# Two hybrid attention layers on one core: input read in 2 KB rows and transposed raw, narrow first modulation blocks, low-rank inputs with features as rows

## The chip, the cores and the metric

The kernel runs on one core of a Trainium2 chip. The metric is device time in microseconds from the start to the end of one execution; less is better. The core has a matrix engine (TensorE, in the profile PE, with its weight loads as PEld), a vector engine (VectorE, DVE), a scalar engine (ScalarE, ACT), GpSimd (POOL), and SyncE (SP), whose queue issues nearly all DMA transfers here, strictly in order.

## What is computed

Two layers of a diffusion backbone over 512 latent tokens `x` and 256 context tokens `ctx`, 2048 features each. A layer modulates its normalised input, projects it once to all head groups and a gate, attends in three groups, and projects back. Cut to what matters:

```
shift, scale, gate = split(silu(c) @ w_ada[l] + b_ada[l], 3)        # also for c_ctx
h  = rms(x, norm_w[l]) * (1 + scale) + shift                          # 512 tokens
hc = rms(xc, norm_w[l]) * (1 + scale_c) + shift_c                     # 256 tokens
u  = h @ w_in[l]      # columns: qa ka va | qb kb vb | cq (768) ckv (512) kpe (64) | z (2048)
qc  = rms_heads(rms(cq, qa_norm) @ w_qb)
kvc = rms(ckv, kva_norm) @ w_kvb
o_a = neighbourhood attention, 8 heads x 64      (latent keys in a window + context keys)
o_b = sliding window, 12 query / 4 kv heads x 64 (sink logit, rotary)
o_c = latent attention, 6 heads, 128 + 64        (all keys)
x   = x + gate * ((concat(o_a, o_b, o_c) * silu(z)) @ w_out[l])
```

In layer 0 the context tokens go the same way, reading context keys alone; in layer 1 only the latent tokens are needed at the end, and so cq, the queries and the gate are computed for 512 tokens, keys and ckv for all 768. Everything is float32.

## The kernel before

**Arithmetic.** To reach float32 precision every matrix product is made of three matmuls of a reduced float type: each operand is split into a high part `hi` and a rest `lo`, and hi*hi, hi*lo, lo*hi are added in PSUM. ACT makes `hi` (a rounding copy), DVE makes `lo` (a subtraction). The helper `Kern.mm` (line 333) issues all of these matmuls, `Kern.tr` (336) all transposes by TensorE; the lines in the profile are those of such helpers (233 `act`, 239 `tt`, 254 and 256 `ts`, 261 `stt`, 266 `red`, 272 `ttr`, 277 `recip`, 282 `pmul`, 303 `start`, which issues a DMA on SP).

**The planner.** The program is written as many small strands (Python generators). A planner, `Weaver`, runs them in a virtual time `vt`, with estimated costs for every instruction, and the order in which it lets them issue is the order of the instructions on each engine and in SP's queue. Strands have priorities (0 goes first). Nothing of this runs on the chip; where an engine there is slower than planned, its instructions still come in the planned order, and a DMA whose buffer isn't free yet holds up all DMAs that stand behind it on SP.

**Memory.** A pool `s3` of 52 tiles (128 x 768) holds nearly all long-lived data: the residual `xk` (16 tiles, one per 128 features), the modulated input `hT` (hi and lo for each of the 16, so 32 tiles), queries, keys, values, staged parts of `w_ada`. `ws`/`wh`/`wl` (3, 3, 2 tiles of 128 x 512) hold weights as loaded, their hi part and their lo part; `tm` are temporaries; `g` are six PSUM banks and `S` two more for scores.

**Weights.** `Kern.loader` (priority 0) takes a free `ws` slot and issues the load of the next piece, `Kern.splitter` makes hi and lo, and a job takes them with `piece`. A `TJob` holds tokens as rows: for each k (128 input features) the stationary operand is a 128 x 128 block of h and 256 columns of weights move; a piece has two k. An `FJob` holds features as rows: a 128 x 128 block of weights is stationary and the tokens move, in two segments of 384 or one of 512; a piece has four k. Each waits, piece by piece, for the h it needs. A `Group` runs several jobs in turn, piece by piece.

**Start.** `load_x` and `load_xk` read x and ctx by feature blocks: for each k one DMA of 4 x 128 rows of 128 floats (512 bytes each) and one of 2 x 128 such rows. ACT squares the 768 columns, DVE sums them to `ssx`. When all 16 are there, `make_h` (once for the latent, once for the context tokens) computes 1/rms into `rx`, and `make_hk` multiplies each block by it (tokens are rows, so it is a scalar per row), transposes it, and, if the modulation for this k isn't known yet, copies it back to `xk`; when it is known, ACT computes hi, DVE or ACT the full value f = scale * x + shift, and DVE lo = f - hi.

The modulation needs `c @ w_ada` for shift and scale, 33.5 MB. `ada_blocks` loads it in DMAs of 256 KB for blocks of 256 columns (rows of 1 KB), shift and scale in turn, staged in up to 12 `s3` tiles; TensorE multiplies them (line 741) with the two columns c and c_ctx stationary, and `ada_finish` (758) transposes the result into place. The block for 256 columns gives two k. The weight loader starts when the first 8 of these loads have been issued. The gate's columns and all of layer 1's modulation follow later on DVE (`ada_vec`, lines 254 and 261, tile `ac`), spread over time.

**Projection.** Jobs for a layer are listed by hand at the end of `layer`. Layer 0 begins with the first half (k 0 to 7) of a key/value chunk and a query chunk of group A, then three gate jobs `zjob` for the heads of group C, then the second halves. A `kv_job` has two key heads and two value heads, a `q_job` up to four blocks of 64 columns: before, two query heads of A and two blocks of cq, or three query heads of B and one block of cq. Two more chunks hold ckv. After a chunk, `post_chunk` copies it from PSUM, squares and sums each 64-column block, applies the head norm (and the rotation for B) and transposes it. For the low-rank blocks ("c") it stores the sums in `ssc`, transposes the raw values and writes them to a DRAM scratch `cscr`.

**Low-rank stage.** `prep_C` reads `cscr` back, feature-major, and splits it with its gain into `cT` (hi, lo), three at a time, each when seven `s3` tiles are free; `prep_norm` computes the norms of cq and ckv from `ssc`. Then `w_qb` and `w_kvb` are applied (`post_qC`, `post_kvC`) and group C's attention runs, and then the output projection, whose `post_out` adds the residual, keeps `xk` for layer 1 and stores it to `xs1`. `free_h` gives back the 32 tiles of h after the last gate job. Attention units run in two worker strands beside the projections.

**Boundary of the layers.** `begin` starts `make_h` for layer 1 before the last output job (context tokens) of layer 0; the 1/rms needs the sums of all 16 blocks.

Of the kernel before, what the change touches and what calls it, by code (L numbers as in the profile page):

```python
# [139 lines left out]
class Kern:  # L140
# [96 lines left out]
    def tt(self, out, a, b, op):  # L237
        yield from self.gate("dve")
        self.nc.vector.tensor_tensor(out, a, b, op=op)  # L239
        self.w.bump("dve", 0.07 + 0.00104 * self.n(out))  # L240

# [133 lines left out]

    def loader(self, go):
# [52 lines left out]
class TJob:  # L429


    def __init__(self, K, W, runs, nk, tiles, lhs, evs, post, room=None, kpp=2, after=None, k0=0):
# [8 lines left out]
        self.inS = False  # L441
# [16 lines left out]
    def step(self, p):  # L458
# [9 lines left out]
        for b, ts in enumerate(self.banks):  # L468
# [8 lines left out]
            if self.evs is not None:  # L477
                yield from K.wait(*(e for x in self.evs[self.k0 + m * p:self.k0 + m * p + m] for e in pick(x, ts[0] < 4, ts[-1] >= 4)))
            yield from K.sync()
            ps = self.ps[b]  # L480
            for kk in range(m):
                k = m * p + kk
                for ti, t in enumerate(ts):
# [5 lines left out]
            K.w.pe(mmc(n) * 3 * m * len(ts))  # L489
# [34 lines left out]
class FJob:  # L524


    def __init__(self, K, W, c0, segs, rhs, evs, post, stack=False, room=None):
# [4 lines left out]
        self.inS = False  # L532
        self.done = [Event() for _ in segs]
# [12 lines left out]
    def step(self, p):  # L546
# [32 lines left out]
        K.drop(hi, lo)  # L579

# [34 lines left out]
def body(K):  # L615
# [8 lines left out]
    one = K.st([128, 1], name="one")  # L624
    nc.vector.memset(one, 1.0)
# [31 lines left out]
    ssc = K.st([128, 6, 20], name="ssc")  # L657
# [169 lines left out]
    def ada_scale(l, n, stag, ptag, depth, group):  # L827
        yield from ada_blocks(l, [(c + o, n) for c in range(0, D, n) for o in (0, D)], stag, ptag, depth, group)
# [20 lines left out]
    ev_x = [(Event(), Event()) for _ in range(KT)]  # L849
    hT = [[None] * KT, [None] * KT]  # L850

    def load_x():
        for k in range(KT):
            xk[k] = yield from K.get("s3")
            w.spawn(load_xk(k), 0)

    def load_xk(k):
        v = xk[k].rearrange("p (t f) -> p t f", f=128)
        yield from K.load(v[:, 0:4], t["x"][0, :, k * 128:(k + 1) * 128].rearrange("(t p) f -> p t f", p=128))
        yield from K.load(v[:, 4:6], t["ctx"][0, :, k * 128:(k + 1) * 128].rearrange("(t p) f -> p t f", p=128), 131072)  # L860
        sq = yield from K.get("s3")
        yield from K.act(sq, xk[k], AF.Square)
        yield from K.red(ssx[:, k, :], sq.rearrange("p (t f) -> p t f", f=128))
        K.put("s3", sq)
        K.set(ev_x[k][0])
        K.set(ev_x[k][1])

    def make_h(l, evs, ev_h, seg):

        a, b = ((0, 4), (4, 6))[seg]  # L870
        yield from K.wait(*(e[seg] for e in evs))
        tot = yield from sm()
        yield from K.red(tot[:, :b - a], ssx[:, :, a:b].rearrange("p k t -> p t k"))
        yield from K.rsqrt(rx[:, a:b], tot[:, :b - a], 1.0 / D)
        K.put("sm", tot)
        for k in range(KT):
            yield from K.token(("hl", "hc")[seg])
            w.spawn(make_hk(l, k, ev_h, seg, a, b), 2)
            yield None

    def make_hk(l, k, ev_h, seg, a, b):
        v = xk[k].rearrange("p (t f) -> p t f", f=128)
        c = slice(a * 128, b * 128)
        n = (b - a) * 128
        yield from K.mul(v[:, a:b], v[:, a:b], rx[:, a:b, None].to_broadcast([128, b - a, 128]))
# [5 lines left out]
        src = ps[:, :n]  # L891
        early = any(e.t is None for e in (ev_sh[l][k], ev_sc[l][k]))
        if early:
            yield from K.act(xk[k][:, c], src)
            src = xk[k][:, c]
            K.put("g", ps)
            K.put(("hl", "hc")[seg], 0)
        yield from K.wait(ev_sh[l][k], ev_sc[l][k])
# [8 lines left out]
        yield from K.act(hi, src, AF.Identity, scale=sc, bias=sh)  # L907
# [1239 lines left out]
```

## Time and profile before

| | |
|---|---|
| median of 3 runs | 2937.42 us (2935.22 to 2939.45) |
| the profiled execution | 2933.86 us, of which 2932.0 from the first to the last instruction (its span) |
| granted TensorE clock, mean | 0.989 |
| PE, PEld busy | 96%, 90% of the span |
| DVE, ACT, POOL busy | 69%, 42%, 5% |
| DMA | 350.09 MB, 119 GB/s over the span |
| costliest group | 7976 matmuls with `wh` moving, 1641.9 us busy (they overlap) |

Times of the views are in microseconds from the start of the span, unless marked ns. A busy matmul is a pipelined one: its duration is longer than the distance to the next, so rates are read from the distance between starts, or from stretches of the chain. PEld is the loading of the stationary operand. Where the profile names a tile, its number is left out: `g` is any of the six PSUM banks, `s` any tile of `s3`, and "L741 PE MATMUL g<-s,scT" is a modulation matmul. The chain is followed back from the last instruction: at each step to what released it.

### The profile page before, as it was taken

How to read it: one execution, taken by the hardware profiler on the slowest of the kernel's cores; microseconds unless marked ns; L12 is line 12 of the kernel's file. 1: busy time of each engine (PE TensorE's matmuls, PEld its weight loads, DVE VectorE, ACT ScalarE, POOL GpSimd, SP SyncE). 2: the span in 40 equal slices, each digit the busy share in tenths (PEclk: the TensorE clock that was granted, in tenths of full speed). 3: DMA queues.
4: the chain of work that ended last, by engine and by line, in shares of the span. 5: the costliest groups of instructions: out<-in, count | busy, mean ns of one | idle time of the engine just before them, and what ended most of it. 6: DMA issues, size and time to landing. Idle time of an engine off the chain costs nothing.

```text
span 2932.0 us, 54116 instructions
## 1 busy us (share of the span) xinstructions
PE 2808.8 (96%) x20218; PEld 2645.5 (90%) x20218; DVE 2013.5 (69%) x5277; ACT 1237.3 (42%) x2692; POOL 148.5 (5%) x221
## 2 busy tenths in 40 slices
PE   5999999999999999989999999999999999999998
PEld 3779999999999999979998789999998999889987
DVE  6247776676887878989964385666667686488643
ACT  5223443342543554546421263434444455356421
POOL 3000100000111001000000000000000000000000
PEclk9999999999999999999999999999999999999999
DMA  9764433433323234323443453444342423412253
GB/s 263 248 193 122 115 107 112 116 95 111 90 81 98 85 109 148 121 75 128 144 135 118 126 156 103 116 116 117 92 116 67 114 84 103 137 45 85 90 176 118
DMA packets 408119, 350.09 MB, mean 119 GB/s; under 512 B 66532, under 2 KB 336914, under 8 KB 407856
## 3 DMA queue, kind: packets, MB, share of 16 engines
q1 hardware_dynamic: 405984, 345.32, 39.6%
q8 instruction: 159, 2.61, 0.4%
q0 software_dynamic: 1872, 1.32, 0.4%
q14 instruction: 104, 0.85, 0.1%
HBM read 305.01 MB, written 32.07 MB: 115 GB/s over the span
## 4 chain that ended last, share of the span: by engine, by line
PE 79%; DVE 11%; DMA 5%; SPq 2%; issue 2%; ACT 2%; DVEq 0%; ACTq 0%
PE g L333 63%; PE S L333 9%; PE g L336 5%; DMA s<-w_ada 2%; SPq L303 2%; DVE s L239 2%; DVE wl L239 2%; DVE s L272 2%; DMA s<-scr 1%; ACT s L233 1%; DVE pt L239 1%; DVE ac L261 1%; DVE s L261 1%; DVE tm L239 1%; PE g L799 1%
## 5 line engine op out<-in xcount | busy, mean ns | idle before, releaser
L333 PE MATMUL g<-wh,s 128*128 128x256 f32 (+2 forms) x7976 | 1641.9, 295 | 15.7 <-DVE s L239 4.7
L333 PEld LDWEIGHTS g<-wh,s 128*128 128x128 f32 x7976 | 1303.6, 192 | 43.1 <-issue 10.0
L333 PE MATMUL g<-wl,s 128*128 128x256 f32 (+2 forms) x3988 | 1167.6, 293 | 5.3 <-DVE wl L239 5.2
L333 PEld LDWEIGHTS g<-wl,s 128*128 128x128 f32 x3988 | 767.0, 192 | 20.0 <-DVE wl L239 11.0
L239 DVE TENSOR_TENSOR wl<-ws,wh 128x512 fp32r<-128x512 f32 (+1 forms) x606 | 413.3, 683 | 490.2 <-PE g L333 292.8
L233 ACT ACTIVATE wh<-ws 128x512 fp32r<-128x512 f32 (+2 forms) x614 | 377.5, 616 | 450.5 <-PE g L333 393.8
L333 PE MATMUL g<-s,wh 128*128 128x384 f32 (+1 forms) x1600 | 451.2, 357 | 1.1 <-DVE s L239 0.6
L233 ACT ACTIVATE s<-s,sm 128x512 f32<-128x512 f32 (+3 forms) x260 | 192.5, 740 | 392.9 <-DVE sm L272 323.3
L261 DVE SCALAR_TENSOR_TENSOR ac<-wa,scT,ac 128x512 f32<-128x512 f32 x420 | 312.4, 761 | 6.8 <-DMA wa<-w_ada 6.2
L333 PEld LDWEIGHTS g<-s,wh 128*128 128x128 f32 x1600 | 293.3, 188 | 24.7 <-issue 2.1
L333 PE MATMUL g<-s,wl 128*128 128x384 f32 (+1 forms) x736 | 261.5, 355 | 0.1
L333 PE MATMUL S<-s,s 128*128 128x256 f32 (+3 forms) x1260 | 235.5, 316 | 13.7 <-DVE sm L272 11.0
L336 PE MATMUL g<-ident,s 128*128 128x128 f32 x1488 | 226.8, 279 | 16.7 <-DVE s L256 8.2
L233 ACT ACTIVATE tm<-g 128x512 f32<-128x512 f32 (+3 forms) x298 | 146.5, 513 | 211.6 <-PE g L333 127.9
L333 PE MATMUL g<-pt,s 128*128 128x256 f32 (+1 forms) x1348 | 217.4, 290 | 16.1 <-DVE pt L239 12.2
L239 DVE TENSOR_TENSOR pt<-g,pt 128x512 fp32r<-128x512 f32 (+1 forms) x306 | 187.6, 623 | 55.6 <-ACT pt L233 54.1
L233 ACT ACTIVATE pt<-g 128x512 fp32r<-128x512 f32 (+1 forms) x306 | 159.8, 543 | 128.4 <-PE g L336 122.9
L333 PEld LDWEIGHTS S<-s,s 128*128 128x128 f32 x1260 | 187.3, 192 | 29.6 <-DVE sm L272 17.5
L333 PEld LDWEIGHTS g<-pt,s 128*128 128x128 f32 x1348 | 186.4, 195 | 24.1 <-DVE pt L239 17.2
L336 PEld LDWEIGHTS g<-ident,s 128*128 128x128 f32 x1488 | 174.7, 143 | 31.9 <-DVE s L256 11.2
L282 POOL TENSOR_TENSOR s<-ot,s 64x256 f32<-64x256 f32 x100 | 87.2, 873 | 1471.9 <-DVE ot L239 1383.8
L333 PEld LDWEIGHTS g<-s,wl 128*128 128x128 f32 x736 | 138.9, 189 | 10.0 <-DVE wl L239 0.8
(156 smaller groups left out, 2483.7 us busy)
## 6 DMA issues: line engine op xcount, KB each, us to landing
wa<-w_ada SPq DMA_DIRECT2D x256, 256.0 KB
ws<-w_in SPq DMA_DIRECT2D x328, 128.0 KB
ws<-w_in SPq DMA_DIRECT2D x160, 256.0 KB
ws<-w_out SPq DMA_DIRECT2D x144, 256.0 KB
s<-w_ada SPq DMA_DIRECT2D x128, 256.0 KB
s<-scr SPq DMA_DIRECT2D x36, 384.0 KB
ws<-w_in SPq DMA_DIRECT2D x64, 192.0 KB
ws<-w_qb SPq DMA_DIRECT2D x54, 192.0 KB
```

The source lines that it names most:

```text
L233: self.nc.scalar.activation(out, in_, func, bias=bias, scale=scale, **kw)
L239: self.nc.vector.tensor_tensor(out, a, b, op=op)
L261: self.nc.vector.scalar_tensor_tensor(out, a, s, b, op0=op0, op1=op1)
L272: self.nc.vector.tensor_tensor_reduce(out, a, b, -1.0, init, OP.add, OP.min, acc)
L282: self.nc.gpsimd.tensor_tensor(out, a, b, op=OP.mult)
L303: self.nc.sync.dma_start(out, in_)
L333: self.nc.tensor.matmul(out, l, r, start=start, stop=stop, skip_group_check=True)
L336: self.nc.tensor.transpose(out, in_, self.ident)
L799: nc.tensor.matmul(pt[:, 2 * c + m:2 * c + m + 1], a[:, c * 128:(c + 1) * 128], one, start=c == 0 and m == sides[0], stop=c == n // 128 - ...
```

## The change

1. *Input.* `load_x` reads quarters of the features: for each quarter six DMAs of 128 tokens x 512 features (rows of 2 KB). ACT squares each with an accumulated sum into `ssx`; `turn_x` transposes the raw blocks and DVE copies them into `xk`, feature-major. `make_h` no longer multiplies before the transpose: it spreads 1/rms over all partitions (a diagonal matrix, multiplied by a matrix of ones on TensorE) into one `s3` tile R. `make_hk` is now f = x * scale * R (DVE), hi = f + shift (ACT), lo = f + shift - hi (DVE). In layer 1 `turn` transposes each block raw when its residual is there, before 1/rms is known.
2. *Modulation.* The first two blocks of 256 columns are cut in two blocks of 128 each (shift and scale), so k = 0 needs 8 loads, of 512-byte rows. The first two jobs of layer 0 wait for h one k at a time (`fine`).
3. *Loader.* While the first modulation runs, the planner places each weight load 2.5 us later (`margin`).
4. *Low-rank inputs.* cq and ckv leave the chunks. `cjob` projects 128 of their features with features as rows, like a gate job, and writes the result to `cscr` without a transpose. `prep_one` squares what it reads back, adds the squares over the feature blocks, and the new `prep_norm` sums them over partitions with one-column matmuls, for cq and ckv apart. Query chunks now hold four heads each (two jobs in A, three in B).
5. *Order.* The list of jobs is written out anew, with the ten `cjob`s between the chunks of groups A and B. `free_h` gives tiles back after each quarter of the last gate job. In `post_out` the store of the residual stands before the events that release the next layer.

```
-        yield from ada_blocks(l, [(c + o, n) for c in range(0, D, n) for o in (0, D)], stag, ptag, depth, group)
+        cols = [(0, 128), (128, 128)] + [(c, n) for c in range(n, D, n)]
+        yield from ada_blocks(l, [(c + o, n) for c, n in cols for o in (0, D)], stag, ptag, depth, group)
...
     def loader(self, go):
...
             s = yield from self.get("ws")
+            w.cur.ft += self.margin
             yield from sp["load"](s)
...
     def load_x():
+        for c in range(4):
+            st = []
+            for i in range(6):
+                x = yield from K.get("s3")
+                w.cur.ft = w.vt
+                src = t["x"][0, i * 128:(i + 1) * 128] if i < 4 else t["ctx"][0, i * 128 - 512:i * 128 - 384]
+                tx = yield from K.load_ahead(x[:, :512], src[:, c * 512:(c + 1) * 512])
+                st.append((x, tx))
+            w.spawn(use_x(c, st), 0)
...
     def make_hk(l, k, ev_h, seg, ev_t, tr):
...
-        yield from K.act(hi, src, AF.Identity, scale=sc, bias=sh)
...
-        yield from K.sub(lo, f[:, :n], r32(hi))
+        yield from K.stt(f[:, :n], xk[k][:, c], sc, bcast[l][1][:, c], OP.mult, OP.mult)
+        yield from K.act(hi, f[:, :n], AF.Identity, bias=sh)
+        yield from K.stt(lo, f[:, :n], sh, r32(hi), OP.add, OP.subtract)
...
-    def free_h():
-        for k in range(KT):
+    def free_h(p):
+
+        for k in range(4 * p, 4 * p + 4):
...
+        def cjob(f):
+
+            sg = segs if f < 6 or not last else [(0, 384), (384, 768)]
+
+            def post(ps, done):
+                for i, (a, b) in enumerate(sg):
+                    yield from K.wait(done[i])
+                    u = yield from K.get("tm")
+                    yield from K.act(u[:, :b - a], ps[i][:, :b - a])
+                    K.put("g", ps[i])
+                    yield from K.store(cscr[f * 128:(f + 1) * 128, a:b], u[:, :b - a], 512 * (b - a))
+                    K.put("tm", u)
+                K.set(ev_c[f])
+            return FJob(K, W, COL["cq"] + f * 128, sg, rhs_h, ev_h, post)
...
+        attA(0,1)
+        jobs.extend([zjob(1), kv_job(GA, "A", 2), cjob(6)])
+        attA(2,3)
+        jobs.extend([q_job(GA, "A", range(4, 8)), zjob(2), kv_job(GA, "A", 4)])
+        attA(4,5)
+        J(lambda: w.spawn(prep_B(), 1))
+        jobs.extend([cjob(7), kv_job(GA, "A", 6), zjob(3)])
+        attA(6,7)
+        jobs.extend([kv_job(GB, "B", 0), zjob(4), zjob(5), q_job(GB, "B", range(0, 4))])
+        attB(0,1,2,3)
+        jobs.extend([cjob(8), cjob(9), cjob(0), zjob(6), q_job(GB, "B", range(4, 8))])
+        attB(4,5)
+        jobs.extend([kv_job(GB, "B", 2), zjob(7)])
+        attB(6,7)
+        jobs.extend([cjob(1), zjob(8), cjob(2), q_job(GB, "B", range(8, 12)), zjob(9)])
+        attB(8,9,10,11)
+        jobs.extend([cjob(3), cjob(4), cjob(5)])
...
-        J(free_h)
+        jobs[-1].after = free_h
...
     def modulation():
         yield from ada_scale(0, 256, "s3", "g", 12, 4)
+        K.margin = 0.0
         w.spawn(ada_rest(), 5)
```

More of the change, by code (lines that the diff above doesn't have):

```diff
@@ L579, in step @@
         K.drop(hi, lo)
+        if self.after is not None:
+            self.after(p)
     def run(self):
@@ L864, in load_xk @@
         K.put("s3", sq)
[L865 to L879, printed above, removed]
@@ L881, in make_hk, with turn_x @@
-    def make_hk(l, k, ev_h, seg, a, b):
+        for e in ev_x[c]:
+            K.set(e)
+    def turn_x(k, seg, st, left):
+        a, b = SEG[seg]
+        w.cur.ft = max(tx for _, tx in st[a:b])
+        yield from K.token(("hl", "hc")[seg])
+        ps = yield from K.get("g")
+        yield from K.sync()
+        o = k % 4 * 128
+        for i in range(a, b):
+            K.tr(ps[:, (i - a) * 128:(i - a + 1) * 128], st[i][0][:, o:o + 128])
+        w.pe(0.109 * (b - a))
+        left[seg] -= 1
+        if left[seg] == 0:
+            K.put("s3", *(x for x, _ in st[a:b]))
+        yield from K.copy(xk[k][:, a * 128:b * 128], ps[:, :(b - a) * 128])
+        K.put("g", ps)
+        K.put(("hl", "hc")[seg], 0)
+        K.set(ev_t0[k][seg])
@@ L882, in make_hk, with turn @@
+    SEG = ((0, 4), (4, 6))
+    bcast = {}
+    def turn(l, k, seg, ev, ev_t):
+        a, b = SEG[seg]
+        yield from K.wait(ev)
+        yield from K.token(("hl", "hc")[seg])
         v = xk[k].rearrange("p (t f) -> p t f", f=128)
         c = slice(a * 128, b * 128)
[L884 to L885 removed]
         ps = yield from K.get("g")
@@ L1615, in prep_one, with prep_norm @@
             K.put("ck", 0)
+            yield from K.act(raw[:, :n], raw[:, :n], AF.Square)
+            if f == 0:
+                squares[key] = raw
+            else:
+                yield from K.wait(ev_sq[key, f - 1])
+                yield from K.add(squares[key][:, :n], squares[key][:, :n], raw[:, :n])
+                K.put("s3", raw)
+            K.set(ev_sq[key, f])
+            if f == nf - 1:
+                w.spawn(prep_norm(key, n // 128), 2, w.cur.ft)
+        def prep_norm(key, nt):
+            q = squares[key]
+            ps = yield from K.get("g")
+            yield from K.sync()
+            for ti in range(nt):
+                nc.tensor.matmul(ps[:, ti:ti + 1], q[:, ti * 128:(ti + 1) * 128], one, start=ti == 0, stop=ti == nt - 1,
+                                 skip_group_check=True)
+            w.pe(0.22 * nt)
+            K.put("s3", q)
+            if key == "q":
+                yield from K.ts(rq_eps[:, 0:nt], ps[:, 0:nt], 1.0 / 768, OP.mult, EPS, OP.add)
+                yield from K.ts(rq_eps[:, 0:nt], rq_eps[:, 0:nt], EPS, OP.mult)
+                K.set(ev_rq)
+            else:
+                yield from K.rsqrt(rkv, ps[:, 0:6], 1.0 / 512)
+                K.set(ev_rkv)
+            K.put("g", ps)
         def room_qC(p):
```

226 lines of the change are left out of this document (114 added, 112 removed).

## The prediction

> **What bounds the kernel now.** I read the page first: the engine totals and the chain that ended last.
>
> ```profile
> PE 2808.8 (96%) x20218; PEld 2645.5 (90%) x20218; DVE 2013.5 (69%) x5277; ACT 1237.3 (42%) x2692; POOL 148.5 (5%) x221
> PE 79%; DVE 11%; DMA 5%; SPq 2%; issue 2%; ACT 2%; DVEq 0%; ACTq 0%
> ```
>
> TensorE carries 79% of the chain. So a saving is either matmul time taken off TensorE, or a stretch in which TensorE stood waiting. The second kind is found by stage (columns: stretch, its length, then PE, PEld, DVE, ACT, POOL busy, granted clock, DMA share, GB/s).
>
> ```profile
> 0.00:50.00 50.00, 17.07 (x135) 11.29 (x135) 33.13 (x75) 26.16 (x48) 21.68 (x43) 1.00 1.01 274
> 100.00:150.00 50.00, 47.37 (x368) 37.57 (x367) 15.93 (x36) 16.59 (x30) 0.00 (x0) 1.00 0.74 230
> 150.00:200.00 50.00, 44.17 (x306) 33.30 (x305) 20.16 (x44) 12.85 (x25) 0.30 (x2) 0.97 0.70 220
> 200.00:250.00 50.00, 50.00 (x380) 49.97 (x379) 27.98 (x58) 10.47 (x22) 0.00 (x0) 1.00 0.42 122
> 800.00:850.00 50.00, 43.93 (x260) 40.80 (x261) 42.56 (x138) 25.51 (x72) 6.68 (x7) 0.86 0.21 61
> 1150.00:1200.00 50.00, 45.11 (x265) 42.93 (x264) 37.80 (x89) 24.04 (x49) 8.12 (x15) 0.93 0.63 193
> 2200.00:2250.00 50.00, 46.29 (x348) 44.45 (x348) 37.65 (x109) 24.83 (x65) 2.92 (x4) 0.93 0.23 67
> ```
>
> From 200 us on TensorE is full, and it loses a few microseconds only at stage changes (800, 1150, 2200). The first 200 us are different: weight loads (PEld) fill 34 to 38 of 50 us there, against 50 afterwards. Since TensorE is full behind this stretch, a microsecond won in it should stay won.
>
> **1. The low-rank inputs (cjob).** The 1280 columns of cq and ckv are now computed in token-major chunks (256 columns moving, 16 x 3 matmuls for each 128 tokens). Layer 0 has 5 such chunks' worth, 5 x 16 x 3 x 6 = 1440 matmuls; layer 1 has 3 for four token tiles and 2 for six, 1152. These 2592 go. In their place stand feature-major jobs: 10 in layer 0 and 4 in layer 1 with two pieces of 384 tokens, 14 x 96 = 1344 matmuls, and 6 in layer 1 with 512 tokens, 288. Prices from stretches of the chain in which TensorE ran one shape after another (start, length, what):
>
> ```profile
> 270.58 2.88 PE g L333 x24
> 311.69 4.17 PE g L333 x24
> 2486.39 54.60 PE g L333 x238
> 825.29 0.87 PE g L336 x8
> ```
>
> 24 matmuls of 256 columns in 2.88 us are 0.120 each, 384 columns 4.17/24 = 0.174, 512 columns 54.60/238 = 0.229, a transpose 0.87/8 = 0.109. So 2592 x 0.120 = 311.0 becomes 1344 x 0.174 + 288 x 0.229 = 299.8: 11.2 us less. The Trainium skill's "TensorE: Matmul & The Clock Gate", section "Wait — 56ns, not 53.3ns?", has a fixed cost of only about 2.5 ns per warm matmul. By its figures the same exchange would be worth an estimated 2.5 us; the three rows here show about 13 ns above 2.4 columns per ns, so the measurement decides.
>
> The transposes of the raw chunk go as well: 10 column blocks x 6 tiles in layer 0, 6 x 4 + 4 x 6 in layer 1, 108 x 0.109 = 11.8 us. The norms return as one-column matmuls (6 + 6 + 6 + 4 = 22), priced by the first row below; the 12 matmuls that spread 1/rms over the partitions have no like, so they lie between the first row (0.116) and the second (9.9/32 = 0.31).
>
> ```profile
> L799 PE MATMUL g<-one,ac 128*128 128x1 f32 x224 | 26.0, 244 | 0.0
> L1394 PE MATMUL g<-tm,flip 128*128 128x256 f32 x32 | 9.9, 389 | 2.3 <-DMA tm<-scr 1.2 <-DMA ws<-w_in 1.0
> ```
>
> 22 x 0.116 = 2.6, and I take the dearer end for the six of layer 1, 1.9; layer 0's six fall where TensorE is idle. TensorE's work falls by 11.2 + 11.8 - 4.5 = **18.5 us**. It counts in full where TensorE is the bound, which the row from 200 us shows; where DVE is the limit (the 800 row) it could be worth half, so 10 to 19.
>
> **2. The start.** The rows that mark it, from the timeline of TensorE (start, length, what, idle before):
>
> ```profile
> 31.89 3.14 PE L741 MATMUL g<-s,scT 128*32 128x256 f32 x16 [22.20 <-DMA s<-w_ada]
> 56.05 0.39 PE L333 MATMUL g<-wh,s 128*128 128x256 f32 x1
> 183.57 0.61 PE L758 MATMUL g<-sel,tm 128*128 128x2 f32 x4 [0.48 <-ACT tm L233]
> ```
>
> Modulation starts at 31.9 us, the first projection at 56.1, and the last modulation block ends at 183.6. What TensorE did between 56 and 184 us, by shape (first and last group of each; 256 columns: 4 groups, 288 matmuls; 384 columns: 4 groups, 216):
>
> ```profile
> L741 PE MATMUL g<-s,scT 128*32 128x256 f32 x418 | 36.5, 394 | 4.5 <-DMA s<-w_ada 3.7
> L333 PE MATMUL g<-s,wh 128*128 128x384 f32 x96 | 27.0, 345 | 0.0
> L333 PE MATMUL g<-wh,s 128*128 128x256 f32 x128 | 26.8, 295 | 2.2 <-DVE s L239 1.2 <-ACT s L233 1.0
> L333 PE MATMUL S<-wl,s 128*128 128x256 f32 x32 | 9.0, 282 | 0.0
> L333 PE MATMUL S<-s,wl 128*128 128x384 f32 x24 | 8.0, 334 | 0.0
> ```
>
> and one group of modulation from the chain of waits:
>
> ```profile
> 120.84 1.00 PE g L741 x16
> ```
>
> With 1.00/16 = 0.0625 for a modulation matmul the work is 288 x 0.120 + 216 x 0.174 + 418 x 0.0625 = 98.3 us of 128: about 30 us of gaps. The projections of the last four k can't run before the last block, so the end of modulation is what moves everything later. It is set by the loads (the stages; the waits of SP's queue up to 200 us: total, times, longest; the DMA issues):
>
> ```profile
> 4.00:26.00 22.00, 1.27 (x5) 0.88 (x5) 10.79 (x13) 11.99 (x19) 13.93 (x27) 1.00 1.05 248
> 30.00:60.00 30.00, 25.67 (x228) 17.32 (x229) 26.30 (x79) 19.09 (x42) 4.57 (x8) 1.00 1.08 337
> 60.00:180.00 120.00, 111.97 (x935) 86.80 (x933) 36.41 (x83) 32.58 (x60) 0.00 (x0) 0.99 0.79 245
> ```
>
> ```profile
> SPq L303 <- DVE wl L239: 45.4, 15, 6.2
> ```
>
> ```profile
> s<-x SPq DMA_DIRECT2D x16, 256.0 KB
> s<-ctx SPq DMA_DIRECT2D x16, 128.0 KB
> ```
>
> The input in 512-byte rows came at 248 GB/s, w_ada mostly in 1 KB rows at 337. The input is 16 x 384 KB = 6.29 MB: 25.4 us at the one rate, 18.7 at the other, so 2 KB rows give about 6.7 (nothing to 8 if they are no faster, or faster still). The narrow first blocks turn 4.2 MB of w_ada into 512-byte rows: 16.9 instead of 12.4 us, 4.5 back. Net 2.2. The Trainium skill's "DMA: Bandwidth & Descriptors", section "Specifications", calls 512 B enough for line rate; by it both terms are nil and the sum is 2.2 us poorer. The rows disagree.
>
> From 60 to 180 us the engines were 79% busy at 245 GB/s. At 337 the same bytes take 87 us: 33 us are lost. The named cause is in the SP row: 15 waits before 200 us, 45.4 us in all, 3.0 each, where a weight load stood at the head of SP's queue for a slot that DVE had not yet split, with w_ada loads behind it. The margin places each weight load 2.5 us later in the plan, so w_ada loads go ahead of it. That can take away at most 15 x 2.5 = 37 us of waits. I take half of the 33, since the 12 staging slots are emptied by TensorE, which is itself at 98 of 128 us: 16.3. **The start: 2.2 + 16.3 = 18.5 us**, between 0 (the waits remain) and 33. Narrow blocks and single-k steps let the first projection begin near 38 us instead of 56: 18.7 for the input, 8 loads of 2.1 MB at 248 GB/s, some 10 for start and the chain of small operations. That fills TensorE earlier, but counts only if the end of modulation comes forward too.
>
> The margin also delays the weights, and TensorE waits for them. Its cover: a piece feeds 4.2 us of matmuls (24 at 0.174, or 36 at 0.120), three slots 12.5 us, of which the margin takes 2.5 and leaves 10 for load and split. Without that cover each of the 28 pieces of this stage could cost 2.5. The single-k step adds a wait on TensorE for every k; behind it in the queue stand the next modulation matmuls, which the pair of k would have held up longer: 0.
>
> **3. Freeing h in quarters.** At the low-rank stage the chain holds
>
> ```profile
> 1159.27 7.45 DMA s<-scr
> ```
>
> a read back of cq that could be issued only when the last gate job gave its 32 tiles up at once. Freed by quarters over a job of about 16 us, three more reads start earlier: **7.5 us**, layer 0 only (0 to 8). The squares moved here (10 of 768 columns per layer on ACT, 9 adds on DVE) lie beside the next round's matmuls; the 1150 row has DVE busy 38 of 50 us. The evictions of the first query round now wait for the query inputs' own norm, after the sixth square; behind them TensorE waits only for the accumulators of a third round, and has 54 matmuls (9.4 us) of the second to do first. Without that cover the last square, add and small matmuls cost 3.
>
> **4. The layer boundary.** There DVE is full and makes h:
>
> ```profile
> 1720.00:1730.00 10.00, 9.16 (x68) 8.44 (x67) 10.00 (x27) 7.23 (x14) 0.00 (x0) 1.00 0.40 111
> L239 DVE TENSOR_TENSOR s<-s,s 128x512 fp32r<-128x512 f32 x16 | 11.0, 687 | 0.9 <-ACT s L233 0.9
> L261 DVE SCALAR_TENSOR_TENSOR ac<-wa,scT,ac 128x512 f32<-128x512 f32 x420 | 312.4, 761 | 6.8 <-DMA wa<-w_ada 6.2
> ```
>
> Two plain 512-column operations per k (0.69 each) become two with a scalar (0.76): 16 x 0.15 = 2.4 us, and 1/rms must first be spread. Against this, transposes run raw before the norm is known, while TensorE waits for the last output chunks. I put it at 0, from -5 to +5. The residual stores move ahead of the event, not ahead of other loads of the same post: 0.
>
> **Sum:** 18.5 + 18.5 + 7.5 = 44.5 us. The profiled execution took 2933.86 (span 2932.0 plus 1.9), so 2889.4; the median of the runs shown is 3.6 higher, hence **2893**.
>
> **The rivals.**
> A. *The start does not get shorter.* SP waits follow how far the chip lags behind the plan; if TensorE and the staging slots set the pace, 2.5 us only moves the waits. For it: waits of up to 6.2 us. Then 2937.4 - 18.5 - 7.5 = 2911. Chance 0.17.
> B. *The start reaches its limit*, loads at 337 GB/s throughout (33 + 2.2), and the stalls at 800 and 2200 us go as group B gets more projection work beside it: about 5 each by the PE column. 2937.4 - 18.5 - 35 - 7.5 - 10 = 2866. Chance 0.13.
> C. *Slower: hand-offs in group B.* Four query heads now come from one job, so four heads' attention is released at once, on DVE. At 800 us one such hand-off cost 6 us of TensorE and a clock of 0.86 over 50 us (7 more): 13. With four hand-offs in each layer so hit, 8 x 13 less the two there now is +78, and the result 2937.4 - 44.5 + 78 = 2971. It decides from four extra stalls. Against it: the new order puts four feature-major jobs, some 67 us, behind the first of them. Chance 0.10.
> D. *The low-rank change is no saving*, the matmuls removed having been beside DVE work anyway, and half the start: 2937.4 - 9 = 2928. Chance 0.05.
>
> **How the numbers follow.** Forecast 0.55, its own range 2878 to 2908. The range for 8 in 10 takes in A and most of the way to B: 2868 to 2922. A measurement here tells 0.2% (6 us) from no change. Faster: forecast, A, B and most of D, 0.87; same 0.04; slower 0.09.
>
> **What would show it.** Right: the first projection near 38 us and the last modulation block at 160 to 170; SP waits for the split well under 45 us before 200; no 256-column chunk of cq; the 7.45 us read gone from the chain near 1100; projections running at 0.174 for the new jobs. Wrong: DMA still near 245 GB/s after 60 us (A), or a PE column below 45 at several places of group B (C).

## The result, and the profile after

The changed kernel takes 2905.89 us (median of four runs, 2902.42 to 2908.11), the kernel before 2936.53 beside it (four runs, 2935.22 to 2939.45). The ratio is 0.9893, 95% interval 0.9876 to 0.991. The profiled execution took 2902.42 us, its span 2900.6. The forecast was 2893 and, for the span, 44.5 us less than before; the span is 31.4 us shorter.

The page after, engine totals and chain shares:

```profile
PE 2794.6 (96%) x19282; PEld 2625.2 (91%) x19282; DVE 1996.1 (69%) x5106; ACT 1199.7 (41%) x2642; POOL 145.8 (5%) x217
PE 78%; DVE 11%; DMA 6%; issue 2%; ACT 2%; SPq 1%; DVEq 0%; ACTq 0%
```

TensorE issues 936 instructions less, and its share of the span is what it was. The stretches that were shown of before, in the same columns:

```profile
100.00:150.00 50.00, 48.48 (x389) 41.51 (x390) 18.36 (x38) 16.84 (x32) 0.00 (x0) 1.00 0.80 247
150.00:200.00 50.00, 45.98 (x321) 38.21 (x320) 23.81 (x45) 12.65 (x25) 0.30 (x2) 0.93 0.57 179
800.00:850.00 50.00, 46.64 (x344) 45.47 (x343) 46.69 (x135) 24.38 (x64) 5.22 (x7) 1.00 0.28 82
1150.00:1200.00 50.00, 47.04 (x315) 44.27 (x314) 48.39 (x152) 29.69 (x76) 0.00 (x0) 1.00 0.41 123
2200.00:2250.00 50.00, 50.00 (x422) 50.00 (x421) 37.33 (x99) 20.51 (x49) 6.30 (x6) 1.00 0.32 91
4.00:26.00 22.00, 14.12 (x76) 11.10 (x77) 11.51 (x24) 14.35 (x45) 12.55 (x24) 0.90 0.96 268
60.00:180.00 120.00, 110.70 (x937) 88.10 (x937) 45.03 (x94) 32.91 (x63) 0.00 (x0) 0.97 0.82 256
```

At 2200 us the loss is gone (PE 46.3 to 50.0); at 800 us 3.4 us of 6.1 are left (PE 43.9 to 46.6), with the clock at 1.00 instead of 0.86. The start's rates have hardly moved: 256 GB/s from 60 to 180 us where there were 245, and the input in 2 KB rows comes at 268 GB/s where there were 248. (e1 and e11 below read the input as before, at 219 and 220 GB/s in the same stretch, so the gain there is 8 to 22%.) TensorE's timeline, and the waits of SP up to 200 us:

```profile
35.85 2.90 PE L958 MATMUL g<-tm,ones 128*128 128x128 f32 x12 [1.19 <-DVE tm L239]
44.52 0.58 PE L338 MATMUL g<-wh,s 128*128 128x256 f32 x1
171.40 1.74 PE L758 MATMUL g<-s,scT 128*32 128x256 f32 x8 [1.50 <-DMA s<-w_ada]
```

```profile
SPq L308 <- DVE wl L239: 38.6, 13, 7.1
```

The first projection begins at 44.5 us (56.1 before), the last modulation matmul starts at 172.5 (182.7). Thirteen waits of SP for a split weight are left, 38.6 us, where there were 15 and 45.4. That fall is no finding: e5 to e9 and e12 run the same instructions up to here and have 39.2 to 45.9 us in 12 or 13 waits. The chain says what the last load of the modulation stood behind:

```profile
162.07 2.19 DVE s L266 x4
164.70 0.62 ACT wh L233
165.35 0.70 DVE wl L239
166.07 0.37 SPq L308
166.49 4.87 DMA s<-w_ada
171.40 1.77 PE g L758 x8
```

VectorE works on h (four operations), then ACT makes the high part of a weight and VectorE its rest, and only then does SP come past the weight load to the `w_ada` load behind it. The wait that the margin was to take away is still the last one.

For the rest the span is cut at four events of SP's and TensorE's timelines: the start of the last modulation matmul of layer 0, the issue of the last load of `w_in`, of `w_kvb` and of `w_out` of layer 0, and of the last load of `w_in` of layer 1. The columns are the lengths between them (us, one profiled execution each).

| kernel | start | projections 0 | low-rank 0 | output 0 | projections 1 | rest | span |
|---|---|---|---|---|---|---|---|
| before | 182.7 | 954.4 | 209.7 | 361.1 | 823.0 | 401.1 | 2932.0 |
| after | 172.5 | 934.0 | 205.9 | 376.2 | 811.6 | 400.4 | 2900.6 |
| e1, low-rank alone | 183.0 | 933.9 | 206.6 | 365.8 | 812.7 | 398.3 | 2900.3 |
| e2, start alone | 174.1 | 956.3 | 212.1 | 368.5 | 814.9 | 401.5 | 2927.3 |
| e3, no margin | 182.7 | 936.9 | 203.8 | 375.6 | 811.3 | 399.1 | 2909.5 |
| e5, old h in layer 1 | 175.6 | 936.9 | 205.5 | 365.8 | 810.5 | 398.1 | 2892.3 |
| e7, h freed at the end | 175.8 | 932.3 | 206.7 | 366.2 | 810.5 | 400.0 | 2891.6 |
| e8, `cjob`s last | 172.9 | 971.1 | 199.6 | 369.4 | 838.1 | 407.6 | 2958.7 |
| e9, e5 and e7 | 177.7 | 937.4 | 200.9 | 357.2 | 809.9 | 397.4 | 2880.6 |
| e11, e1, h freed at the end | 183.7 | 934.7 | 204.8 | 356.8 | 813.8 | 398.2 | 2892.0 |
| e12, e7, late transposes | 176.2 | 936.1 | 204.4 | 358.3 | 815.0 | 399.7 | 2889.7 |

After against before: 10.2 won in the start, 20.4 and 11.4 in the projections, 3.8 in the low-rank stage, 0.7 in the rest, and **15.1 lost in the output stage of layer 0**, on which the prediction had put nothing: 31.4. The start column scatters: after, e5, e7, e8, e9 and e12 are alike up to there and lie from 172.5 to 177.7. So do the others: e7, e9 and e12 hold the same instructions into the output stage, and have 932.3 to 937.4 us in projections 0 and 200.9 to 206.7 in the low-rank stage. A difference of some 5 us in one cell shows nothing by itself.

### The profile page after: what moved, and what is told of

Same layout as the page of the kernel before. It is cut to its first block, busy times and chain, and to the rows that moved or that the text cites. A ratio compares the mean times of both kernels' runs of the same rounds, so it can differ in the third digit from the quotient of the medians.

```text
span 2900.6 us, 51642 instructions
## 1 busy us (share of the span) xinstructions
PE 2794.6 (96%) x19282; PEld 2625.2 (91%) x19282; DVE 1996.1 (69%) x5106; ACT 1199.7 (41%) x2642; POOL 145.8 (5%) x217
## 4 chain that ended last, share of the span: by engine, by line
PE 78%; DVE 11%; DMA 6%; issue 2%; ACT 2%; SPq 1%; DVEq 0%; ACTq 0%
PE g L338 62%; PE S L338 9%; PE g L341 5%; DVE s L266 2%; DVE wl L239 2%; DVE s L239 2%; DVE s L277 1%; DMA s<-scr 1%; ACT s L233 1%; DMA tm<-scr 1%; DVE ac L266 1%; DVE tm L239 1%; SPq L308 1%; PE g L758 1%; PE g L816 1%
## 5 line engine op out<-in xcount | busy, mean ns | idle before, releaser
L338 PE MATMUL g<-wh,s 128*128 128x256 f32 (+2 forms) x6248 | 1312.9, 299 | 17.0 <-DVE s L266 4.7
L338 PEld LDWEIGHTS g<-wh,s 128*128 128x128 f32 x6248 | 1029.1, 193 | 46.1 <-ACT s L233 8.5
L338 PE MATMUL g<-wl,s 128*128 128x256 f32 (+2 forms) x3124 | 924.5, 296 | 5.4 <-DVE wl L239 5.4
L338 PE MATMUL g<-s,wh 128*128 128x384 f32 (+1 forms) x2688 | 763.2, 355 | 0.6 <-ACT wh L233 0.5
L338 PEld LDWEIGHTS g<-wl,s 128*128 128x128 f32 x3124 | 603.3, 193 | 18.1 <-DVE wl L239 9.1
L338 PEld LDWEIGHTS g<-s,wh 128*128 128x128 f32 x2688 | 493.0, 188 | 31.2 <-issue 2.1
L338 PE MATMUL g<-s,wl 128*128 128x384 f32 (+1 forms) x1280 | 449.1, 351 | 0.3 <-DVE wl L239 0.3
L338 PEld LDWEIGHTS g<-s,wl 128*128 128x128 f32 x1280 | 241.4, 189 | 12.7 <-DVE wl L239 0.9
L338 PE MATMUL g<-pt,s 128*128 128x256 f32 (+1 forms) x1348 | 210.4, 286 | 9.5 <-DVE pt L239 5.5
L239 DVE TENSOR_TENSOR pt<-g,pt 128x512 fp32r<-128x512 f32 (+1 forms) x306 | 187.5, 623 | 45.4 <-ACT pt L233 43.5
L341 PEld LDWEIGHTS g<-ident,s 128*128 128x128 f32 x1488 | 176.5, 143 | 37.1 <-DVE s L261 6.3
L233 ACT ACTIVATE tm<-g 128x384 f32<-128x384 f32 (+4 forms) x240 | 113.4, 491 | 206.6 <-PE g L338 129.6
```

Source lines behind the costliest of these rows:

```text
L233: self.nc.scalar.activation(out, in_, func, bias=bias, scale=scale, **kw)
L338: self.nc.tensor.matmul(out, l, r, start=start, stop=stop, skip_group_check=True)
L341: self.nc.tensor.transpose(out, in_, self.ident)
```

## The experiments

The theory after the result: the low-rank part does what it was meant to do and more; the start gives less than forecast; and the output stage loses time to the boundary between the layers, where the raw transposes stand and VectorE has more to do. The rivals: the loss is the new order of the jobs, or the freeing by quarters, or the start's lead is swallowed by some later wait in any case. Kernels that didn't run side by side are compared by their ratios to the kernel before, taken on the same chip.

**e1, the low-rank part alone, and e2, all the rest.** e1 keeps parts 4 and 5 of the change (new jobs and order, quarters) and has input, modulation, margin, h and the residual's store as before; e2 is the complement. Lines of e1 against the whole change:

```
-        self.margin = 2.5
-        cols = [(0, 128), (128, 128)] + [(c, n) for c in range(n, D, n)]
-        yield from K.stt(f[:, :n], xk[k][:, c], sc, bcast[l][1][:, c], OP.mult, OP.mult)
+        yield from K.mul(v[:, a:b], v[:, a:b], rx[:, a:b, None].to_broadcast([128, b - a, 128]))
```

> Only the low-rank jobs, the new order and the freeing by quarters; input, modulation, loader and the making of h as before. By stages of the two profiles the projections of layer 0, the low-rank stage and layer 1 without its boundary gained about 35 us, the start 10, and output projection with boundary lost 14. If these parts add up, this kernel takes 2936.5 - 35 = about 2901, no slower than the whole change. The rival, that the low-rank part gave only the 18.5 + 7.5 of the prediction and the start the rest, expects 2910.

> The complement: new input, narrow blocks, single-k waits, margin, h made with a spread 1/rms in both layers, residual store earlier; low-rank blocks and order as before. If the start's 10 us are given back at the boundary, within 5 us of the kernel before (2932 to 2942). If the start pays by itself as predicted (18.5, boundary 0), 2918. The last modulation block should end near 172 us either way.

e1: 2903.74 us, ratio 0.9904 (0.9882 to 0.9926). e2: 2929.81, ratio 0.9987 (0.9978 to 0.9996). So the low-rank part alone is as fast as the whole change, as far as these intervals tell, and the rest alone is worth about 0.1%. By the table e2 has won 8.6 us when the modulation ends, and loses 7.4 in the output stage of layer 0; the whole change stands 11.1 ahead of e1 at the last load of `w_kvb` (172.5 + 934.0 + 205.9 = 1312.4 against 1323.5) and 0.6 ahead at the last load of `w_out`. The lead is lost inside one stage.

**e3, the margin, and e4, the narrow blocks.**

```
-        self.margin = 2.5
+        self.margin = 0.0
```

```
-        cols = [(0, 128), (128, 128)] + [(c, n) for c in range(n, D, n)]
+        cols = [(c, n) for c in range(0, D, n)]
```

> The whole change with margin 0. If the margin takes SP's waits away, as predicted, the last modulation block ends about 10 us later than the 172 us of the whole change, and the time is 2914 to 2918. If it only moves the waits (they fell from 45.4 to 38.6 us before 200 us), the time stays within 4 us of 2906.

> The whole change with first modulation blocks 256 columns wide. If 512-byte rows of w_ada cost what the prediction took (4.5 us on the end of modulation), this kernel is 2 to 5 us faster, 2901 to 2904. If the early first projection (44.5 us instead of 56.1) is what the start gained, it is 5 to 8 slower, 2911 to 2914.

e3: 2908.74 us, ratio 0.9916 (0.9898 to 0.9934). The last modulation matmul starts at 182.7 again, as before the change and as was expected if the margin works; the time is not the 2914 to 2918 that went with it, and its interval overlaps that of the whole change. SP's waits:

```profile
SPq L308 <- DVE wl L239: 46.4, 15, 7.1
```

So in the profile all that the start won is the margin's; 2 KB rows and narrow blocks alone bring the first projection to 44.1 us and the end of the modulation nowhere. But the margin doesn't win by taking these waits away: 46.4 us here is within 1 us of the 45.9 that e9 has with the margin, and e9's modulation still ends 5 us earlier. What the later weight loads change instead was not traced. e4: 2905.45, ratio 0.9907 (0.9891 to 0.9923), the first projection at 47.8 us and the modulation's end at 174.4, inside the scatter: the narrow blocks can't be told from nothing.

**e5, layer 1's h as before.** Layer 1 multiplies by 1/rms before the transposes again, after the last output chunk of its tokens; ACT makes hi and f from PSUM.

```
-                w.spawn(make_h(l, ev_in[l], ev_h, seg), 2)
+                w.spawn((make_h1 if l else make_h)(l, ev_in[l], ev_h, seg), 2)
```

> The whole change, but layer 1 makes h as before (multiplied, then transposed, f on ACT). In the whole change DVE is full for 40 us at the boundary (10.00 of 10) and TensorE drops to 5.94 of 10 with a clock of 0.84. If this is what took the start's gain back, the stall goes and the kernel is 8 to 11 us faster than 2905.9, 2895 to 2898. If the boundary costs nothing, as the prediction had it, it stays within 4 us.

2888.81 us, ratio 0.9846 (0.983 to 0.9861), against 0.9893 (0.9876 to 0.991) of the whole change: the boundary cost the difference of the ratios, 0.0047 or 13.8 us (by the two intervals, give or take 7). The output stage is down from 376.2 to 365.8.

**e6, the copies of the context's transposes on ACT** instead of VectorE.

```
-        if seg == 0:
-            yield from K.act(xk[k][:, c], ps)
-        else:
-            yield from K.copy(xk[k][:, c], ps[:, :256])
+        yield from K.act(xk[k][:, c], ps[:, :(b - a) * 128])
```

> The whole change; in layer 1 the 16 copies of the context blocks (0.42 us each on DVE) are made by ACT, which is half idle there. If DVE's time alone sets the boundary, 16 x 0.42 = 6.7 us less DVE work, of which the part that falls into the full 40 us (8 of 16 copies, 3.3 us) is won: 2902 to 2904. If the order of DVE's work or the wait for the norm sets it: 2906.

2899.39 us, ratio 0.9885 (0.9869 to 0.9902). That interval overlaps the whole change's in nearly all its width; the run decides nothing.

**e7, h's tiles given back after the last gate job,** as before.

```
-        jobs[-1].after = free_h
+        J(lambda: [free_h(p) for p in range(4)] and None)
```

> The whole change with h's 32 tiles given back after the last gate job, as before. The prediction took 7.5 us for freeing by quarters, so 2913. By the stages of the two profiles the low-rank stage of layer 0 was 3.9 us shorter: 2910. If the read back was hidden by other work in any case: 2906.

2893.29 us, ratio 0.986 (0.9846 to 0.9875): giving the tiles back *later* is faster, by 0.0033 or 9.7 us (give or take 7). In the low-rank stage the chain of e7 holds reads of the scratch again,

```profile
1129.93 5.26 DMA s<-scr
1138.60 10.69 DMA s<-scr
```

which the chain of the changed kernel has not in that stage. So the freeing does take the read away, and the stage is no shorter for it: 205.9 and 205.5 us with quarters (after, e5), 206.7, 200.9 and 204.4 without (e7, e9, e12). The price stands in the next stage, 376.2 us against 366.2, in two places. The changed kernel, in the columns of the stretches, 0 to 30 and 180 to 210 us after the stage's begin:

```profile
1312.40:1342.40 30.00, 27.55 (x197) 26.09 (x196) 27.79 (x81) 18.89 (x42) 1.07 (x2) 0.94 0.37 116
1492.40:1522.40 30.00, 24.50 (x155) 23.32 (x155) 20.66 (x39) 5.46 (x8) 0.00 (x0) 0.77 0.47 136
```

and e7:

```profile
1314.80:1344.80 30.00, 30.00 (x233) 28.95 (x232) 29.55 (x90) 20.59 (x52) 1.06 (x2) 1.00 0.42 125
1494.80:1524.80 30.00, 26.45 (x205) 25.66 (x204) 25.83 (x48) 8.09 (x12) 0.00 (x0) 0.94 0.53 161
```

36 matmuls less in the first 30 us, 50 less in the second. Nothing of what runs there was edited; the freed tiles let the planner start other strands earlier, and from the low-rank stage on the same instructions stand in another order. The changed kernel's second place, in its timeline:

```profile
1498.26 2.42 PE L816 MATMUL g<-ones,ac 128*128 128x1 f32 x16 [1.06 <-DVE tm L239]
1505.86 0.56 PE L338 MATMUL g<-wh,s 128*128 128x256 f32 x1 [1.99 <-DVE tm L239]
1513.03 0.50 PE L338 MATMUL g<-wh,s 128*128 128x256 f32 x1 [2.15 <-DVE tm L239]
```

Three hand-offs stand close together here, and TensorE runs the matmuls between them at half clock (the last section has the clock). e7 has sums of the modulation (the x16 group) of this kind at 1491.8, ahead of the stall. e1 with e11 and e5 with e9 repeat the pair. That the order does it is shown; which of the strands would have to be held back was not tried.

**e8, the `cjob`s behind the last query job of group B** instead of spread between the chunks.

```
-        jobs.extend([cjob(8), cjob(9), cjob(0), zjob(6), q_job(GB, "B", range(4, 8))])
+        jobs.extend([zjob(6), q_job(GB, "B", range(4, 8))])
...
-        jobs.extend([cjob(3), cjob(4), cjob(5)])
+        jobs.extend([cjob(f) for f in (6, 7, 8, 9, 0, 1, 2, 3, 4, 5)])
```

> The whole change with all ten low-rank jobs after the last query job of group B, so that no such job stands between the hand-offs of attention. TensorE's work is the same. If spreading them gave the 8 us of idle time that layer 0's projections lost (the stall at 800 us most of all), this kernel is 8 to 16 us slower over both layers, 2914 to 2922; if a four-head hand-off without filler costs 13 each, as the rival of the prediction had it, 2930 or more; if the order does not matter, 2906.

2961.87 us, ratio 1.0096 (1.0081 to 1.0111): slower than the kernel before, and 0.0203 or 60 us above the whole change. By the table layer 0's projections are 37.1 us longer and layer 1's 26.5. e8 and then the changed kernel, the same stretches:

```profile
650.00:700.00 50.00, 41.41 (x302) 38.51 (x301) 41.80 (x115) 23.84 (x62) 4.01 (x4) 0.90 0.25 75
700.00:750.00 50.00, 45.23 (x332) 42.61 (x333) 46.51 (x133) 24.17 (x60) 7.07 (x7) 0.90 0.23 67
```

```profile
650.00:700.00 50.00, 49.62 (x299) 49.15 (x298) 38.33 (x94) 17.82 (x38) 0.73 (x1) 1.00 0.38 111
700.00:750.00 50.00, 49.91 (x361) 49.18 (x360) 40.47 (x107) 22.43 (x58) 3.65 (x5) 1.00 0.33 101
```

What TensorE waits for most in e8 in these 100 us is VectorE's row maxima of the scores in group B's attention, which begins at 649 us (total, times, longest):

```profile
PE S L338 <- DVE sm L277: 9.4, 8, 2.2
```

All its waits there come to 12.9 us, those of the changed kernel in the same stretch to 0.4. Without feature-major jobs to lie beside attention, TensorE stands 8.6 and 4.8 us and the granted clock falls to 0.90. This is rival C's mechanism, and the order of the jobs is what keeps it away.

**e9, e5 and e7 together; e10, the same with twice the margin; e11, e1 with h freed at the end.** For e10:

```
-        self.margin = 2.5
+        self.margin = 5.0
```

> The whole change with two edits: layer 1 makes h as before (its own modulation, no raw transposes), and h's tiles are freed after the last gate job. Alone the first gave 2888.81 us and the second 2893.29, beside 2905.89 with the whole change: 17 and 12.6 less. Theory that they are two costs, one at the layer boundary and one in the order of the strands of the output stage: they add, 2876 to 2881 us, and the stage from layer 0's last load of w_kvb to its last load of w_out takes some 356 us (366 with either one). Rival, that both take away the same lateness (VectorE at the boundary, which the second relieves by ending the stage's strands in another order): no more than the better one, 2886 to 2891, and that stage stays at 365.

> The same with a margin of 5.0 us, so that the loads of the modulation's weights are issued later still against their buffers' release. Theory that SP's waits (38.6 us in 13 waits with the change) are what is left to win in the start: the last matmul of the modulation of layer 0 comes at 168 to 172 us instead of 172 to 176, and the end 3 to 8 us earlier. Rival, that TensorE's order or the staging sets it by now: within 3 us of the kernel with the margin as it is.

> The low-rank part of the change alone (start, h and margin as before), with h's tiles freed after the last gate job. Theory that the start's 10 us reach the end as soon as the boundary between the layers doesn't take them: this one is 8 to 10 us slower than the whole change with both edits, near 2888 us. Rival, that some later wait swallows the start's lead in any case: within 3 us of it. And if freeing at the end helps by the order of strands alone, it helps here too: some 8 to 12 us below the 2903.74 of the low-rank part alone.

e9: 2882.33 us, ratio 0.9813 (0.9797 to 0.983), the fastest kernel here, 53 us below the kernel before. The time is 1 us above the range in which the two costs add, but by the ratios they do: 0.0047 + 0.0033 = 0.0080, and e9 lies 0.0080 below the whole change. Its output stage takes 357.2 us, as the first theory said. e10: 2883.45, ratio 0.9815 (0.9795 to 0.9835), modulation's end at 177.9 where e9 has 177.7: a larger margin does nothing more that these runs could tell. e11: 2892.32, ratio 0.9853 (0.9833 to 0.9873), 10.0 us above e9 on the same chip: with the boundary out of the way, e9 keeps a lead to the end that fits the start's. (e9 has the moved store of the residual besides, and in these two profiles only 6.0 us of the lead stand when the modulation ends; the stages behind it scatter by as much.) So, as far as this pair shows, the lead isn't swallowed by a later wait: start and boundary are two separate items, one won and one lost. And freeing at the end helps here too, by 0.0051 between e1 and e11, or 15 us (11.4 by the medians). The four output stages with the old or new h, and quarters or not, say the same: 376.2 us (after), 365.8 (e5), 366.2 (e7), 357.2 (e9).

What the boundary does to TensorE, seen in e7 and e9, which differ in nothing else. e7: two stretches before and three after the last load of `w_out`; then, in a fence of its own, the transposes (line 341) alone in the first two (PE busy, clock, DMA):

```profile
1641.00:1661.00 20.00, 19.80 (x115) 16.93 (x114) 8.95 (x23) 9.86 (x19) 0.00 (x0) 1.00 0.45 137
1661.00:1681.00 20.00, 18.92 (x97) 14.07 (x96) 16.21 (x44) 9.51 (x17) 0.00 (x0) 1.00 0.61 172
1681.00:1701.00 20.00, 17.91 (x106) 14.93 (x106) 16.92 (x35) 9.72 (x16) 0.00 (x0) 1.00 0.53 156
1701.00:1721.00 20.00, 19.27 (x138) 17.90 (x138) 20.00 (x49) 10.66 (x20) 0.00 (x0) 1.00 0.40 113
1721.00:1741.00 20.00, 15.87 (x108) 14.99 (x108) 19.52 (x53) 12.29 (x27) 0.30 (x2) 0.91 0.22 61
```

```profile
1641.00:1661.00 20.00, 6.42 (x52) 1.00 0.45 137
1661.00:1681.00 20.00, 5.64 (x36) 1.00 0.61 172
```

e9, the same distance from its last load of `w_out` (1673.3), the three stretches after it and their transposes:

```profile
1673.30:1693.30 20.00, 17.55 (x109) 14.83 (x110) 19.55 (x52) 15.26 (x26) 0.00 (x0) 1.00 0.60 181
1693.30:1713.30 20.00, 20.00 (x157) 19.13 (x156) 19.21 (x48) 17.54 (x29) 0.00 (x0) 1.00 0.33 93
1713.30:1733.30 20.00, 20.00 (x150) 18.93 (x150) 16.76 (x47) 17.19 (x36) 0.31 (x2) 1.00 0.34 96
```

```profile
1673.30:1693.30 20.00, 4.15 (x28) 1.00 0.60 181
1693.30:1713.30 20.00, 6.17 (x44) 1.00 0.33 93
1713.30:1733.30 20.00, 4.03 (x22) 1.00 0.34 96
```

In e7, 52 + 36 = 88 transposes stand between the output matmuls, where TensorE had no time to give away (88 x 0.109 = 9.6 us; the stage is 9.0 longer). Behind it VectorE is busy 16.9, 20.0 and 19.5 of 20 us and TensorE 53.0 of 60; in e9 most transposes lie there, VectorE is about as busy, and TensorE is busy 57.6. What TensorE waits for most in e7 in the 80 us from that point is VectorE (total, times, longest):

```profile
PE g L341 <- DVE tm L239: 4.1, 2, 3.3
```

The groups of VectorE in the same 80 us, e7 first, then e9 (count, busy, mean ns):

```profile
L266 DVE SCALAR_TENSOR_TENSOR s<-s,ada,s 128x512 fp32r<-128x512 f32 x16 | 11.8, 748 | 0.0
L266 DVE SCALAR_TENSOR_TENSOR s<-s,gsc,s 128x256 f32<-128x256 f32 x16 | 7.4, 482 | 0.2 <-ACT s L233 0.2
```

```profile
L239 DVE TENSOR_TENSOR s<-s,s 128x512 fp32r<-128x512 f32 x16 | 10.9, 684 | 0.3 <-ACT s L233 0.3
L239 DVE TENSOR_TENSOR s<-s,rx 128x256 f32<-128x256 f32 x16 | 6.6, 419 | 0.0
```

One operation of each pair is shown; the others are alike. With a scalar, 16 blocks take 0.9 (512 columns) and 0.8 us (256) longer per operation, and there are two operations of each size: 3.4 us, and on top come the copies of the context's transposes, 0.42 each, 16 x 0.42 = 6.7, part of them ahead of the stretch. ACT, which made f before, is busy 9.7 to 12.3 of 20 us in e7's three stretches and 15.3 to 17.5 in e9's.

**e12, e7 with the raw transposes held back until 1/rms is known,** so that they follow the output matmuls while VectorE and ACT do what they do in the change.

```
-        for k in range(KT) if l else ():
-            w.spawn(turn(l, k, seg, evs[k][seg], ev_t[k]), 2)
         yield from K.wait(*(e[seg] for e in evs))
...
+        for k in range(KT) if l else ():
+            w.spawn(turn(l, k, seg, evs[k][seg], ev_t[k]), 2)
```

> The whole change with h's tiles freed at the end (2893.29 us, ratio 0.986), and layer 1's raw transposes started only when 1/rms is known, so that all of them follow the output jobs; what ACT and DVE do for h stays as in the change. With layer 1's h made as before instead, the same kernel took 2882.33 (0.9813). Theory that the boundary loses its time because 88 of the transposes now stand between the output matmuls, where TensorE has no time to spare: the stage from layer 0's last load of w_kvb to its last load of w_out shrinks from 366 to about 357 us, the 60 us after it keep some 53 to 57 us of TensorE, and the time is 2882 to 2886. Rival, that VectorE's longer work for h is the loss (h = two operations with a scalar of 0.75 us each, and copies): what the output stage gains is lost again behind it, where VectorE is full, and the time stays at 2891 to 2896.

2891.52 us, ratio 0.985 (0.9835 to 0.9865): e7's interval overlaps it, and it is clear above e9's (0.9797 to 0.983). The output stage does what the first theory said, 358.3 us instead of 366.2, and in the 60 us behind it TensorE is busy 59.4 us, more than in e9 (57.6). But layer 1's projections take 815.0 us against 810.5 in e7 and 809.9 in e9, a difference at the edge of the scatter. One wait of TensorE there is new:

```profile
PE g L1451 <- DMA tm<-scr: 3.1, 1, 3.1
```

in the 50 us from 1825, where e9 has no wait at all. In the 80 us after the last load of `w_out`, VectorE is busy 71.4 us, in e9 63.8. So the place of the transposes accounts for the output stage, and moving them back does not win the time back. The time is the rival's, yet TensorE waits for VectorE only 0.7 us in those 80 (2.5 in e9), so it isn't shown that VectorE is what takes the rest. What of the boundary's 13.8 us each part of the new h costs stays open.

## Why the prediction was right, and where it failed

The time (2905.89) lies in the range and in the forecast's own, 2878 to 2908, by 2 us. That is luck as much as judgement: the sum is made up otherwise than the steps said. By the ratios, of 2935 us, the low-rank inputs gave 43 us instead of 18.5 and the start 12 instead of 18.5, freeing in quarters lost 10 instead of winning 7.5, and the boundary lost 14 instead of nothing. One error of 25 us stands against three of 38 together.

**Step 1, the low-rank inputs (18.5): the work as counted, the worth undersized.** In e11 the matmuls of 256 columns are 2592 fewer, those of 384 and 512 columns 1344 and 288 more, the transposes 108 fewer, all as counted; only the one-column matmuls are 44 more, since each of the 22 in the program is two instructions in the trace, some 2.5 us more at 0.116. The rates stand in the chain of the changed kernel:

```profile
295.04 2.87 PE g L338 x24
317.42 4.17 PE g L338 x24
```

0.120 and 0.174 again. Against the work of layer 0's projections (1440 x 0.120 + 60 x 0.109 - 960 x 0.174 = 12.3 us) the stage shrinks by 19.7 in e11. The other 7.4 fit the stall at 800 us (in e11 PE 46.6 of 50 us and a clock of 0.97), which the prediction had given to rival B alone. In all e11 is 0.0147 or 43 us below the kernel before, where the prediction had 18.5. By the table the remainder lies in the low-rank stage (4.9 us less than before), the output stage (4.3) and the rest (2.9); what won it there was not traced. Each of these is within what a single cell scatters. (The prediction's estimate of the exchange at 2.5 ns a matmul should be 960 x 2.5 ns = 2.4 us, not 2.5.)

**Step 2, the start (18.5): half.** The modulation ends at 175.1 us on the mean of after, e5, e6 (174.8), e7, e8, e9 and e12, at 183.1 on that of before, e1 and e11: 8.0 earlier; at the end it is worth 10.0 by the times of e11 and e9, 12 by their ratios. Failed in it: "That can take away at most 15 x 2.5 = 37 us of waits." With the margin the waits come to 38.6 to 45.9 us in the seven profiles of that mean, 42.4 on average; without it to 43.4 to 46.4 in before, e1, e3 and e11, 45.2 on average; with twice the margin to 42.2. Some 3 us were taken away where 16.3 were forecast (half of the 33 would be 16.5), and how the rest of the 8 was won was not found. What holds SP at the last load is VectorE, behind its own work on h, as the chain at 162 us shows. The term of the rates failed too: 2 KB rows came at 268 GB/s, not 337. The Trainium skill's "DMA: Bandwidth & Descriptors", section "Specifications", calls 512 B enough for line rate. By that there is no gain. Measured are 8 to 22% (248, 219 and 220 GB/s in rows of 512 bytes), between none and the prediction's 36%. First projection: 44.5 us, not 38; the input's last block landed at 29.4 us, and the chain from there by 1/rms, its spreading (12 matmul instructions in 2.90 us, at a clock of 0.50) and the first modulation blocks took 15, not 10. The waits for h one k at a time and the moved store of the residual were not run apart.

**Step 3, freeing in quarters (7.5): the read goes, the time doesn't.** The stage is no shorter than in e7, e9 and e12, and 9.7 us are lost overall. The step asked what is late next in the low-rank stage, not what the freed tiles would let the planner start.

**Step 4, the boundary (0, from -5 to +5): the step that failed most,** 13.8 us lost. The prediction let "transposes run raw before the norm is known, while TensorE waits for the last output chunks": TensorE doesn't wait there. It waits behind it, for VectorE (1.6 us in 80 in the kernel before, which has transposes there, and 4.1 for one kind of result in e7, which has moved them ahead). And the 2.4 us of VectorE counted only the two operations of the latent half, not the context's and not the copies. How the 13.8 us divide between these is open (e12).

**The rivals.** A (the start stays) has a time, 2911, near the result, and its sign came: 256 GB/s after 60 us, hardly above 245. But the start moved by 8. B's start did not come; of its stalls the one at 2200 us went and half of that at 800. C is real and was rightly judged: e8 shows it at 60 us (the prediction had 78), and the order that "puts four feature-major jobs, some 67 us, behind the first of them" is what keeps it away. D fell, by e1 and e11. Of the prediction's own signs for being right, the read gone from the chain and the jobs at 0.174 came; the first projection at 38 us, the last modulation block at 160 to 170 and waits well under 45 us did not.

## What to carry to other kernels

Work that is moved ahead of a wait is free only if the engine is idle at the place it is moved to; look at that stretch, not at the wait. Count an operation for every segment it is made of, and ask which engine did it before. Where a planner writes the order, a resource that comes free earlier is a new order, and its effect stands further on than the stage it was meant for; time it alone. And before a cell of a stage table is read, see how far kernels that are alike up to there scatter in it.

## What the runs showed of the hardware

A short stall costs more than its length. The clock granted to TensorE in the changed kernel around the hand-offs at 1498 us (stretches of 2 us):

```profile
1496.00:1498.00 2.00, 1.19 (x11) 0.99 (x9) 1.93 (x4) 0.00 (x0) 0.00 (x0) 1.00 0.36 104
1500.00:1502.00 2.00, 1.74 (x9) 1.66 (x9) 0.33 (x2) 0.00 (x0) 0.00 (x0) 0.50 0.05 16
1506.00:1508.00 2.00, 2.00 (x10) 2.00 (x11) 1.97 (x4) 0.91 (x2) 0.00 (x0) 0.50 0.83 136
1518.00:1520.00 2.00, 2.00 (x19) 2.00 (x18) 1.65 (x3) 0.93 (x2) 0.00 (x0) 1.00 0.75 234
```

After a wait of 1.06 us, followed by one-column matmuls, the clock is 0.50 from 1500 on: ten matmuls fall into 2 us instead of nineteen (one of 256 columns every 0.21 us instead of every 0.12), and with two more waits of 2 us it is not at 1.00 for good before 1518. The Trainium skill's "TensorE: Matmul & The Clock Gate", section "Part 1: The HAM clock gate (the "warmup" mystery)", names an idle window of about 3.4 us before the clock is halved. Here no single wait was that long. Whether one-column matmuls count as idle there, no run here shows.
